# A transformer layer on one core: the order of weighing and turning in attention, the first products, and matmuls ahead of the last scaling

## The chip, the cores and the metric

The kernel runs on one core of one Trainium2 chip. Its five engines each work through their own list of instructions: TensorE (PE; its weight loads are shown as PEld) multiplies matrices into the accumulator memory PSUM, VectorE (DVE), ScalarE (ACT) and GpSimd (POOL) do the elementwise work, and SyncE (SP) issues the DMA transfers between the chip's main memory and the on-chip memory. Semaphores order them against one another. The metric is the device time of one execution in microseconds (us).

## The reference

One layer of an encoder over two request groups that share the weights (512 and 1024 tokens, width 1024), all in float32:

```python
a = _rmsnorm(h, norm_mix_g)
z = a @ w_in                                  # q, k, v and u, 1280 columns
o_attn = _attention(q, k, v, q_norm_g, k_norm_g)   # 8 heads, 2 for k and v, axial rotary, softmax
o_pool = _pool_mixer(u, w_pool, pool_scale)
h = h + jnp.concatenate([o_attn, o_pool], axis=-1) @ w_out
m = _rmsnorm(h, norm_mlp_g)
h = h + jnp.square(jax.nn.relu(m @ w_up)) @ w_down
gate = jax.nn.sigmoid((_rmsnorm(h, norm_ple_g) @ w_ple_gate).astype(jnp.float32)).astype(h.dtype)
h = h + gate * (p_i @ w_ple_proj)
return _rmsnorm(h, final_norm_g)
```

## The kernel before

Every operand of a product is split into a high part (rounded to the type fp32r) and a low part (the rest), and a product of two operands is three products on PE: high by high, high by low, low by high. The splitting (a copy or cast on ACT, a subtraction on DVE or POOL) is most of the elementwise work. The order of PE, ACT, DVE and POOL is written out by hand; SP's follows the order in which loads and stores are written and the semaphores that they wait for. Data tiles lie in 49 equal slots that are handed on as they come free.

**Start.** Eight bf16 products of a constant tile (`warm`) run on PE while the first data comes. The tokens lie in 12 tiles of 128. `z` of a tile is a sum over 8 blocks `k` of 128 input features, and a block is nine products: six of 512 columns (weights `W1`, two column ranges) and three of 256 (weights `W2`). `mm_k(t, k)` issues the nine products of tile t and block k. Tiles 0 and 1 run together over k, since the weights only arrive then: `load_w(k)` issues the loads, `split_w(k)` splits the weights (ACT, then DVE), `load_x` and `split_x` do the same for the tokens. Of tiles 0 and 1 the features of blocks 0 and 1 (`head`) come first, the rest (`tail`) later.

**Attention.** A unit is one tile of 128 queries with the 4 query heads of one k/v head. The loop over `at` works in rounds, four to a unit. A round issues the score `S` of one head (`score`; DVE takes its maximum), the exponential of the round before (`soften`, ACT), its division by the sum (`norm`, POOL), the turn of finished probabilities `pr` (`turn`: four PE transposes into a PSUM buffer `tp` for each 128 keys; there are two such buffers), the split of the turned ones into `pt` (`split`: high part on ACT, rest on DVE, which frees the buffer), and the weighing of the values with the `pt` of the round before (`weigh`: PE adds into the accumulator `o`). A unit of the first request group has 4 key tiles, one turned in each round; a unit of the second has 8, two in each round. A round can end with a piece of other work from the queue `fill`: of `pool_out` (products `pp`, first 48 pieces of six products) or of `heads_out` (products `po`, 12 of 256 columns, for a pair of tiles whose heads are done). In the rounds with `at` from 62 to 95 a piece is taken only in some even ones. Where the variable `filled` is true, a round weighs first and then turns; otherwise it turns first. It is true from round 3 on as long as `fill` holds anything, whether or not the round takes a piece.

**End.** After the MLP and the gate, the last group of tokens (256) is normalised in `finish`. `rsqrt_rows` sums the squares `sq` over the features on PE (`ss`), in two parts since the last one comes late, raises the mean to the power -1/2 (DVE, POOL), puts it on a diagonal (`dg`, DVE) and spreads it to all partitions with one product (`bc`). DVE then multiplies five parts of the result by `bc`, which lies in PSUM, and SP stores each.

Of the kernel before, what the change touches and what calls it, by code (L numbers as in the profile page):

```python
# [9 lines left out]
F32 = mybir.dt.float32  # L10
F32R = mybir.dt.float32r
AF = mybir.ActivationFunctionType
ALU = mybir.AluOpType
# [22 lines left out]
def encoder_layer(ctx, tc, xT, xn, xr, pT, w1, w2, w_pool, w_out, w_up, w_down, w_gate, w_proj,  # L36
# [18 lines left out]
    def load(dst, src):  # L55
        ins = sy.dma_start(dst, src).ins
        if last_pe[0] is not None:
            tc.add_manual_dep(ins, last_pe[0].name, NOSYNC, reason="not before its turn")
# [79 lines left out]
    w2raw = {}  # L138
    gmix_sb = const.tile([P, KD], F32, name="gmix_sb")

    def load_w(k):
        raw = slot([P, D], F32, f"w1r{k}")
        for part in ([slice(0, CH), slice(CH, D)] if k == 0 else [slice(0, D)]):
            load(raw[:, part], w1[k][:, part])
        if k % 2 == 0:
            w2raw[k // 2] = slot([P, 2, 256], F32, f"w2r{k}")
            load(w2raw[k // 2], w2[k // 2])
            w2t = slot([P, 2, 2, 256], F32R, f"w2_{k}")
            W2[k], W2[k + 1] = [[w2t[:, b, i] for i in range(2)] for b in range(2)]
        W1[k] = [slot([P, D], F32R, f"w1_{k}_{i}") for i in range(2)]  # L150
        return raw, w2raw[k // 2][:, k % 2]

    def split_w(k, raws):
        g = gmix_sb[:, k:k + 1]
        parts = [(raws[0], W1[k]), (raws[1], W2[k])]
        if k == 0:
            parts[:1] = [(raws[0][:, h], [w[:, h] for w in W1[k]]) for h in (slice(0, CH), slice(CH, D))]
        for r, W in parts:
            sc.activation(W[0], r, AF.Copy, scale=g)  # L159
            ve.scalar_tensor_tensor(W[1], r, g, as32(W[0]), op0=ALU.mult, op1=ALU.subtract)  # L160

# [1 line left out]
    wz = slot([P, CH], mybir.dt.bfloat16, "warm")  # L163
    gp.memset(wz, 1.0)
    wps = tp_ps("warm")
    for i in range(8):
        pe.matmul(wps, wz[:, 0:P], wz, start=True, stop=True)
    ones_sb = const.tile([P, P], F32R, name="ones_sb")
    gp.memset(as32(ones_sb), 1.0)
# [1 line left out]
    load(gmix_sb, g_mix)  # L171
    head, tail = slice(0, 2), slice(2, KD)
    x0 = load_x(0, (head,))
    raws = [load_w(0)]
    x1 = load_x(1, (head,))
    raws += [load_w(1)]
    for t, x in ((0, x0), (1, x1)):
        load(x[:, tail], xT[t][:, tail])
        raws.append(load_w(2 + t))
    split_x(0, x0, head)  # L180
    split_w(0, raws[0])
    split_x(1, x1, head)
    split_w(1, raws[1])
    split_x(0, x0, tail)
    split_w(2, raws[2])
# [42 lines left out]

    zs = {}

    def mm_k(t, k):
        if k == 0:
            zs[t] = ps("z", f"z{t}")
        z = zs[t]
        hi = [(i, j, 0) for j in range(3) for i in range(2)] if k == 0 and t < 2 else [(i, j, 0) for i in range(2) for j in range(3)]
        lo = [(0, j, 1) for j in range(3)]
        for i, j, w_ in (hi[:3] + lo + hi[3:] if k else hi + lo):
            w = W2[k][w_] if j == 2 else W1[k][w_][:, j * CH:(j + 1) * CH]
            pe.matmul(z[:, j * CH:min((j + 1) * CH, 1280)], xt[t][i][:, k, :], w,
                      start=k == 0 and i + w_ == 0, stop=k == KD - 1 and i == 1)  # L240
# [331 lines left out]
    def step(n=1):  # L572
# [5 lines left out]
        while n and chores:  # L578
            try:
# [2 lines left out]
            except StopIteration:  # L582
                chores.popleft()

    def rsqrt_rows(parts, w, name):

        n = w // P
        ss = tp_ps(f"ss{name}")
        for i, part in enumerate(parts):
            for b in range(n):  # L590
                pe.matmul(ss[:, b:b + 1], part[:, b * P:(b + 1) * P], as32(ones_sb[:, 0:1]),
                          start=i + b == 0, stop=i == len(parts) - 1, skip_group_check=True)
        r = small.tile([P, 4], F32, tag="rs", name=f"rs{name}", bufs=2)
        ve.tensor_scalar(r[:, :n], ss[:, :n], 1.0 / D, EPS, op0=ALU.mult, op1=ALU.add)
        if name in ("g0", "g1"):
            yield
        gp.tensor_tensor(r[:, :n], r[:, :n], mhalf[:, :n], op=ALU.pow)
        spread = [P, n, P]
        if len(parts) > 1:
            dg = slot([P, w], F32, f"dg{name}")  # L600
            ve.tensor_tensor(dg.rearrange("p (a b) -> p a b", a=n), id_sb.unsqueeze(1).to_broadcast(spread),
                             r[:, :n].unsqueeze(2).to_broadcast(spread), op=ALU.mult)
            bc = tp_ps(f"bc{name}")
            pe.matmul(bc[:, :w], as32(ones_sb), dg, start=True, stop=True)
            return bc[:, :w]
        rh = small.tile([P, 2, 4], F32R, tag="rh", name=f"rh{name}", bufs=2)
        gp.tensor_scalar(rh[:, 0, :n], r[:, :n], 1.0, 1.0, op0=ALU.mult, op1=ALU.mult)
        gp.tensor_tensor(rh[:, 1, :n], r[:, :n], as32(rh[:, 0, :n]), op=ALU.subtract)
        dg = slot([P, 2, w], F32R, f"dg{name}")
        if name in ("g0", "g1"):  # L610
            yield from wait(2)
        for i in range(2):
            ve.tensor_tensor(dg[:, i].rearrange("p (a b) -> p a b", a=n), id_sb.unsqueeze(1).to_broadcast(spread),
                             as32(rh[:, i, :n]).unsqueeze(2).to_broadcast(spread), op=ALU.mult)
        yield from wait({"f20": 4, "g2": 8, "f00": 7, "f10": 4}.get(name, 3))
        bc = tp_ps(f"bc{name}")
        for i in range(2):
            pe.matmul(bc[:, :w], ones_sb, dg[:, i], start=i == 0, stop=i == 1)
        return bc[:, :w]
# [594 lines left out]
            at_join(n, join_product, g, h)  # L1214
            at_join(n + 3, join_store, g, h)
    start_chunk(0)
    for k in range(KD - 2):
        mm_k(0, k)
        mm_k(1, k)
    mm_k(0, KD - 2)  # L1220
# [75 lines left out]
    for at in range(2, 4 * len(units) + 6):  # L1296
# [26 lines left out]
        if last:  # L1323
            last[0].norm(last[1])
            if last[1] == 3:
                n = last[0].n
                turning += [[(last[0], kt) for kt in range(i * n // 4, (i + 1) * n // 4)] for i in range(4)]
        filled = bool(fill) and at >= 3
        if filled:
            done = [un_ for un_, kt in lag if un_.weigh(kt)]  # L1330
        for un_, kt in fresh:
# [5 lines left out]
        if not filled:  # L1337
            done = [un_ for un_, kt in lag if un_.weigh(kt)]

        n = 0 if at < 3 else 2 - at % 2 if at < first_sample else 1  # L1340
        took = n and bool(fill)
        for i in range(max(n, 1)):
            if i == n - 1 or not n:
# [347 lines left out]
    def finish(c, o, w, sq):  # L1691
        tok = slice(o, o + w)
        if not o:
            yield from wait((2, 4, 3)[c])
        bc = yield from rsqrt_rows(sq, w, f"f{c}{o}")
        if o:
            for a, part in ((0, slice(0, 1)), (0, slice(1, 2)), (1, slice(0, 2)), (2, slice(0, 2)), (3, slice(0, 2))):
                h = res(c, 2 * a + part.start, tok, 2)[:, 0:part.stop - part.start]
                ve.tensor_tensor(h, h, bc.unsqueeze(1).to_broadcast([P, part.stop - part.start, w]), op=ALU.mult)
                sy.dma_start(y_out[c, a][:, part, tok], h)  # L1700
            return
        r = slot([P, w], F32, f"fr{c}{o}")
        sc.copy(r, bc)
        yield from wait(2)
        for a in range(4):
            for e in range(2):
                h = res(c, 2 * a + e, tok)
                ve.scalar_tensor_tensor(h, h, gfin_sb[:, 2 * a + e:2 * a + e + 1], r, op0=ALU.mult, op1=ALU.mult)  # L1708
                if not e:
                    yield  # L1710
            sy.dma_start(y_out[c, a][:, :, tok], hT[c][a][:, :, tok] if c < 2 else res(c, 2 * a, tok, 2))
            yield
# [127 lines left out]
```

## Time and profile before

| | |
|---|---|
| median of 3 runs | 1744.55 us (1744.01 to 1744.94) |
| the profiled execution | 1746.53 us |
| its span, first to last instruction | 1744.8 us |
| mean granted TensorE clock | 0.997 |
| first products of z | from 5.48 us |
| rounds of attention | 186 to 536 us |
| MLP | 561 to 1592 us, overlapping the gate |
| gate and last norm | 1543 to 1745 us |

All times in the profile count from the start of the span. A row of the timeline gives start, duration, engine, line, operation, out<-in, shape and count, and in brackets the idle time before it with what ended it. Rows of the same operation are drawn together while the engine does not stand still. A row of the list of waits gives who waited for whom, the total, how often, and the longest. A row of the windows gives the stretch and its length, then busy time and (count) of each engine, the granted clock, the DMA engines' share and GB/s. A row of the groups gives the count, the busy time in total, the mean duration in ns, and the idle time before them. The ends of matmuls are modelled: of a stream of matmuls the starts tell more than the durations.

### The profile page before, as it was taken

What the parts mean: (1) busy time and instruction counts of PE and PEld (TensorE: products, weight loads), DVE (VectorE), ACT (ScalarE), POOL (GpSimd) and SP (SyncE); (2) the same over time, 40 slices, a digit from 0 to 9 for tenths busy, and PEclk for the clock granted to TensorE, in tenths of its full rate; (3) what the DMA queues carried; (4) which work ended last, traced back from release to release, by engine and by line L of the source; (5) the groups of instructions that cost most, each with busy time, mean ns of one, the idle gap of its engine ahead of it and who ended that gap; (6) DMA issues with size and microseconds to landing.
All of it is one profiled execution on the core that took longest, in us unless ns stands there. A gap on an engine that the chain in (4) does not pass through costs nothing. (4 is left out here: it accounts for less than half of the span.)

```text
span 1744.8 us, 31256 instructions
## 1 busy us (share of the span) xinstructions
PE 1716.8 (98%) x11684; PEld 1568.6 (90%) x11684; DVE 1262.5 (72%) x1724; ACT 886.9 (51%) x1605; POOL 1072.9 (61%) x870
## 2 busy tenths in 40 slices
PE   9999999999999999999999999999999999999997
PEld 7888878888878998888989999999999999998897
DVE  5777765777886668677757777777778788675666
ACT  5454354667885545554445455544454445533233
POOL 1585984434665766868546677866588577653422
PEclk9999999999999999999999999999999999999998
DMA  7354745120428887979797978779776888853012
GB/s 257 133 203 161 264 159 190 63 97 13 145 79 334 305 298 266 364 287 349 295 377 286 351 240 328 270 279 368 253 262 244 298 284 315 295 188 115 13 49 97
DMA packets 137063, 400.16 MB, mean 229 GB/s; under 512 B 14544, under 2 KB 27216, under 8 KB 136912
## 3 DMA queue, kind: packets, MB, share of 16 engines
q1 hardware_dynamic: 136912, 398.17, 62.6%
q8 instruction: 92, 1.51, 0.3%
q14 instruction: 59, 0.48, 0.1%
HBM read 280.15 MB, written 117.96 MB: 228 GB/s over the span
## 5 line engine op out<-in xcount | busy, mean ns | idle before, releaser
L49 PE MATMUL pd<-ta,v 128*128 128x256 f32 x2688 | 338.4, 282 | 0.1
L49 PEld LDWEIGHTS pd<-ta,v 128*128 128x128 f32 x2688 | 328.3, 190 | 0.7 <-POOL v L1098 0.3
L1098 POOL TENSOR_TENSOR v<-we,v 128x512 fp32r<-128x512 f32 x128 | 184.8, 1465 | 102.0 <-DVE ta L1118 37.8
L49 PE MATMUL pd<-r,wd 128*128 128x512 f32 x768 | 189.7, 395 | 1.6 <-DVE r L1015 1.3
L1098 POOL TENSOR_TENSOR v<-vs,v 128x512 fp32r<-128x512 f32 x96 | 127.5, 1350 | 96.9 <-DVE c L1121 32.5
L49 PE MATMUL z<-w,x 128*128 128x512 f32 (+1 forms) x864 | 176.8, 362 | 1.7 <-ACT w L159 1.7
L505 POOL TENSOR_SCALAR pr<-pr,rr 128x1024 f32<-128x1024 f32 (+1 forms) x96 | 94.7, 987 | 134.7 <-DVE rr L503 72.2
L1118 DVE TENSOR_TENSOR ta<-c,ta 128x512 fp32r<-128x512 f32 x112 | 116.9, 1044 | 78.0 <-ACT ta L1116 73.8
L49 PEld LDWEIGHTS z<-w,x 128*128 128x128 f32 x864 | 145.0, 191 | 28.6 <-ACT w L159 3.6
L49 PEld LDWEIGHTS pd<-r,wd 128*128 128x128 f32 x768 | 139.7, 188 | 31.4 <-DVE r L1015 3.1
L909 POOL TENSOR_TENSOR w<-ws,w 128x512 fp32r<-128x512 f32 x72 | 107.8, 1498 | 93.5 <-ACT w L908 87.3
L49 PE MATMUL pq<-mo,w 128*128 128x256 f32 x1152 | 152.3, 281 | 5.1 <-DVE c L1050 2.9
L49 PE MATMUL pz<-mo,w 128*128 128x256 f32 x1152 | 152.6, 282 | 0.8 <-DVE u L1045 0.8
L49 PE MATMUL px<-mo,w 128*128 128x256 f32 x1152 | 152.5, 282 | 0.0
L49 PEld LDWEIGHTS pz<-mo,w 128*128 128x128 f32 x1152 | 145.7, 189 | 4.1 <-DVE u L1045 1.2
L49 PEld LDWEIGHTS pq<-mo,w 128*128 128x128 f32 x1152 | 143.1, 189 | 6.1 <-DVE c L1050 3.3
L49 PEld LDWEIGHTS px<-mo,w 128*128 128x128 f32 x1152 | 144.4, 189 | 1.4
L515 ACT CAST pt<-tp 128x512 fp32r<-128x512 f32 x160 | 87.8, 590 | 111.4 <-PE tp L53 109.7
L49 PE MATMUL pg<-hg,wg 128*128 128x512 f32 (+1 forms) x768 | 141.2, 338 | 0.2 <-DVE hg L1438 0.2
L516 DVE TENSOR_TENSOR pt<-tp,pt 128x512 fp32r<-128x512 f32 x160 | 104.2, 685 | 48.1 <-ACT pt L515 48.1
L49 PEld LDWEIGHTS pg<-hg,wg 128*128 128x128 f32 x768 | 119.2, 188 | 17.0 <-DVE hg L1438 0.4
L489 DVE TENSOR_REDUCE nm<-S 128x1 f32<-128x1024 f32 (+1 forms) x96 | 100.1, 1043 | 22.4 <-PE S L49 21.9
(257 smaller groups left out, 3506.7 us busy)
## 6 DMA issues: line engine op xcount, KB each, us to landing
w<-kept_d SPq DMA_DIRECT2D x210, 512.0 KB, 6.0
kept_d<-w SPq DMA_DIRECT2D x105, 512.0 KB, 4.4
we<-in_w_down_dram SPq DMA_DIRECT2D x64, 512.0 KB, 6.8
mo_d<-mm SPq DMA_DIRECT2D x84, 256.0 KB, 5.8
mo<-mo_d SPq DMA_DIRECT2D x42, 512.0 KB, 10.0
wur<-in_w_up_dram SPq DMA_DIRECT2D x36, 512.0 KB, 8.2
wdr<-in_w_down_dram SPq DMA_DIRECT2D x32, 512.0 KB, 6.4
h_d<-h SPq DMA_DIRECT2D x16, 512.0 KB, 2.9
```

The costliest lines, as they stand in the source:

```text
L49: last_pe[0] = nc.tensor.matmul(*a, **k).ins
L489: ve.tensor_reduce(nm, S[:, :nch * CH], axis=AX.X, op=ALU.max, negate=True)
L505: gp.tensor_scalar(p, p, rr, 1.0, op0=ALU.mult, op1=ALU.mult)
L515: sc.copy(self.pt[kt][:, 0], tp)
L516: ve.tensor_tensor(self.pt[kt][:, 1], tp, as32(self.pt[kt][:, 0]), op=ALU.subtract)
L909: gp.tensor_tensor(t[:, 1], x, as32(t[:, 0]), op=ALU.subtract)
L1098: ins = gp.tensor_tensor(lo[:, p], src[:, p], as32(hi[:, p]), op=ALU.subtract).ins
L1118: last_ve[0] = ve.tensor_tensor(t[:, 1], x, as32(t[:, 0]), op=ALU.subtract).ins
```

## The change

Four places change.

- The first products. `mm_first` replaces the first blocks of tiles 0 and 1. It goes by column ranges: all six products on `W1` of tile 0, then of tile 1, then the three on `W2` of each. Tile 1's load is issued ahead of the load of `W2`, and its split ahead of that of `W2`. The number of `warm` products goes from 8 to 10.
- Attention. `filled` is now true only in rounds that will take a piece of `fill`; all other rounds turn first and weigh after. Round 3 takes two pieces in place of one.
- `rsqrt_rows` issues 14 products of `ones_sb` with itself (128 columns) between the two parts of the sum, and 11 ahead of the product that spreads it, in the one call that has two parts.
- `finish`: for the last group ACT copies the spread factors to `r`, and POOL multiplies the last part (two feature tiles of 256 tokens) by `r`, while DVE does the other four. Its store is issued fourth.

```diff
-    def load_w(k):
+    def load_w(k, between=lambda: None):
         raw = slot([P, D], F32, f"w1r{k}")
         for part in ([slice(0, CH), slice(CH, D)] if k == 0 else [slice(0, D)]):
             load(raw[:, part], w1[k][:, part])
+        W1[k] = [slot([P, D], F32R, f"w1_{k}_{i}") for i in range(2)]
+        other = between()
         if k % 2 == 0:
...
-    def split_w(k, raws):
+    def split_w(k, raws, between=lambda: None):
...
         for r, W in parts:
+            if W is W2[k]:
+                between()
             sc.activation(W[0], r, AF.Copy, scale=g)
...
-    for i in range(8):
+    for i in range(10):
         pe.matmul(wps, wz[:, 0:P], wz, start=True, stop=True)
...
-    raws = [load_w(0)]
-    x1 = load_x(1, (head,))
+    raws = [load_w(0, lambda: load_x(1, (head,)))]
+    x1 = raws[0][2]
...
-    split_w(0, raws[0])
-    split_x(1, x1, head)
+    split_w(0, raws[0], lambda: split_x(1, x1, head))
...
+    def mm_first():
+        for js in ((0, 1), (2,)):
+            for t in range(2):
+                if t not in zs:
+                    zs[t] = ps("z", f"z{t}")
+                for i, j, w_ in [(i, j, 0) for j in js for i in range(2)] + [(0, j, 1) for j in js]:
+                    w = W2[0][w_] if j == 2 else W1[0][w_][:, j * CH:(j + 1) * CH]
+                    pe.matmul(zs[t][:, j * CH:min((j + 1) * CH, 1280)], xt[t][i][:, 0, :], w,
+                              start=i + w_ == 0, stop=False)
...
+    def keep_warm(n, name):
+        wp = ps_g("g", name)
+        for _ in range(n):
+            pe.matmul(wp[:, 0:P], ones_sb, ones_sb, start=True, stop=True)
...
         for i, part in enumerate(parts):
+            if i:
+                keep_warm(14, f"wa{name}")
...
+            keep_warm(11, f"wb{name}")
             bc = tp_ps(f"bc{name}")
...
-    for k in range(KD - 2):
+    mm_first()
+    for k in range(1, KD - 2):
         mm_k(0, k)
         mm_k(1, k)
...
-        filled = bool(fill) and at >= 3
+        filled = bool(fill) and at >= 3 and (at < 62 or at % 2 == 0 and (at < 76 or at % 3 or len(fill) > 10) or at >= 96)
...
-        n = 0 if at < 3 else 2 - at % 2 if at < first_sample else 1
+        n = 0 if at < 3 else 2 if at == 3 else 2 - at % 2 if at < first_sample else 1
...
         if o:
-            for a, part in ((0, slice(0, 1)), (0, slice(1, 2)), (1, slice(0, 2)), (2, slice(0, 2)), (3, slice(0, 2))):
+            r = slot([P, w], F32, f"fr{c}{o}")
+            sc.copy(r, bc)
+            for a, part in ((0, slice(0, 1)), (3, slice(0, 2)), (0, slice(1, 2)), (1, slice(0, 2)), (2, slice(0, 2))):
+                e, by = (gp, r) if a == 3 else (ve, bc)
                 h = res(c, 2 * a + part.start, tok, 2)[:, 0:part.stop - part.start]
-                ve.tensor_tensor(h, h, bc.unsqueeze(1).to_broadcast([P, part.stop - part.start, w]), op=ALU.mult)
-                sy.dma_start(y_out[c, a][:, part, tok], h)
+                e.tensor_tensor(h, h, by.unsqueeze(1).to_broadcast([P, part.stop - part.start, w]), op=ALU.mult)
+                if a != 3:
+                    sy.dma_start(y_out[c, a][:, part, tok], h)
+                if a == 1:
+                    sy.dma_start(y_out[c, 3][:, :, tok], res(c, 6, tok, 2))
```

How the order on PE changes at three places. First, PE's first products of z, before. `z_433` is tile 0, `z_443` tile 1; `w_0_0` and `w_0_1` are the high and low parts of `W1`, `w_0_123` is `W2`; `x_0` and `x_1` are the high and low parts of a tile's tokens.

```order
L49 MATMUL z_433<-w_0_0_124,x_1_146 128x512
L49 MATMUL z_433<-w_0_123,x_0_145 128x256
L49 MATMUL z_433<-w_0_123,x_1_146 128x256
L49 MATMUL z_433<-w_0_1_125,x_0_145 128x512 x2
L49 MATMUL z_433<-w_0_123,x_0_145 128x256
L49 MATMUL z_443<-w_0_0_124,x_0_155 128x512
```

The same place after the change, where `z_435` is tile 0 and `z_442` tile 1, from the last high product on `W1` of tile 0:

```order
L49 MATMUL z_435<-w_0_0_123,x_1_148 128x512
L49 MATMUL z_435<-w_0_1_124,x_0_147 128x512 x2
L49 MATMUL z_442<-w_0_0_123,x_0_155 128x512
L49 MATMUL z_442<-w_0_0_123,x_1_156 128x512
L49 MATMUL z_442<-w_0_0_123,x_0_155 128x512
L49 MATMUL z_442<-w_0_0_123,x_1_156 128x512
L49 MATMUL z_442<-w_0_1_124,x_0_155 128x512 x2
L49 MATMUL z_435<-w_0_129,x_0_147 128x256
```

The products on `W2` stood fifth, ahead of eight products on `W1`; now they stand behind all of those.

Second, PE in a round late in attention that takes no piece of `fill` (`at` is 71), from the last product of its score, before:

```order
L49 MATMUL S_13_4994<-ks_1_1611,qb_4353 128x512
L49 MATMUL o_0_4984<-pt_02_4976,vs_941 128x512 x2
L49 MATMUL o_0_4984<-pt_03_4979,vs_941 128x512 x2
L53 MATMUL tp_04_5008<-id_sb,pr_00_4774 128x128
L53 MATMUL tp_04_5008<-id_sb,pr_01_4813 128x128
L53 MATMUL tp_04_5008<-id_sb,pr_02_4849 128x128
L53 MATMUL tp_04_5008<-id_sb,pr_03_4883 128x128
L53 MATMUL tp_05_5013<-id_sb,pr_00_4774 128x128
L53 MATMUL tp_05_5013<-id_sb,pr_01_4813 128x128
L53 MATMUL tp_05_5013<-id_sb,pr_02_4849 128x128
L53 MATMUL tp_05_5013<-id_sb,pr_03_4883 128x128
L49 MATMUL S_00_5032<-ks_0_939,qb_4738 128x512
```

And after:

```order
L49 MATMUL S_13_4996<-ks_1_1613,qb_4355 128x512
L53 MATMUL tp_04_5006<-id_sb,pr_00_4776 128x128
L53 MATMUL tp_04_5006<-id_sb,pr_01_4815 128x128
L53 MATMUL tp_04_5006<-id_sb,pr_02_4851 128x128
L53 MATMUL tp_04_5006<-id_sb,pr_03_4885 128x128
L53 MATMUL tp_05_5011<-id_sb,pr_00_4776 128x128
L53 MATMUL tp_05_5011<-id_sb,pr_01_4815 128x128
L53 MATMUL tp_05_5011<-id_sb,pr_02_4851 128x128
L53 MATMUL tp_05_5011<-id_sb,pr_03_4885 128x128
L49 MATMUL o_0_4986<-pt_02_4978,vs_943 128x512 x2
L49 MATMUL o_0_4986<-pt_03_4981,vs_943 128x512 x2
L49 MATMUL S_00_5034<-ks_0_941,qb_4740 128x512
```

The weighing of key tiles 2 and 3 moved behind the turn of key tiles 4 and 5. The same holds in all 15 rounds that take no piece between `at` 71 and 93, in round 95, whose weighing then stands directly ahead of round 96's, and in round 52, whose piece was taken a round earlier. From round 3 to round 52 each piece of `fill` after the first stands one place earlier in the queue than before; where two pieces share a round, the rounds' pieces read alike.

Third, PE's end, before (`ssf` is the sum of squares, `bcf` the spread product):

```order
L49 MATMUL pg_19832<-hg_1_19142,wg_0_18585 128x256
L49 MATMUL pg_19832<-hg_0_19141,wg_1_18586 128x256
L49 MATMUL ssf_19870<-ones_sb,s_19546 128x1 x2
L49 MATMUL ssf_19870<-ones_sb,s_19860 128x1 x2
L49 MATMUL bcf_19880<-dgf_19878,ones_sb 128x256
```

And after:

```order
L49 MATMUL pg_19834<-hg_0_19143,wg_1_18588 128x256
L49 MATMUL ssf_19872<-ones_sb,s_19548 128x1 x2
L49 MATMUL waf_19875<-ones_sb 128x128 x14
L49 MATMUL ssf_19872<-ones_sb,s_19862 128x1 x2
L49 MATMUL wbf_19897<-ones_sb 128x128 x11
L49 MATMUL bcf_19909<-dgf_19895,ones_sb 128x256
```

One new group stands ahead of the second ssf, the other ahead of bcf.

More of the change, by code (lines that the diff above doesn't have):

```diff
@@ L149, in load_w @@
             W2[k], W2[k + 1] = [[w2t[:, b, i] for i in range(2)] for b in range(2)]
-        W1[k] = [slot([P, D], F32R, f"w1_{k}_{i}") for i in range(2)]
-        return raw, w2raw[k // 2][:, k % 2]
-    def split_w(k, raws):
+        return raw, w2raw[k // 2][:, k % 2], other
+    def split_w(k, raws, between=lambda: None):
         g = gmix_sb[:, k:k + 1]
@@ L234, in mm_k @@
         z = zs[t]
-        hi = [(i, j, 0) for j in range(3) for i in range(2)] if k == 0 and t < 2 else [(i, j, 0) for i in range(2) for j in range(3)]
+        hi = [(i, j, 0) for i in range(2) for j in range(3)]
         lo = [(0, j, 1) for j in range(3)]
```

## The prediction

> **What bounds the kernel now.** I read the page's busy line first, then the list of waits for TensorE (PE, and its weight loads PEld).
>
> ```profile
> PE 1716.8 (98%) x11684; PEld 1568.6 (90%) x11684; DVE 1262.5 (72%) x1724; ACT 886.9 (51%) x1605; POOL 1072.9 (61%) x870
> ...
> PE z L49 <- ACT w L159: 1.7, 2, 1.2
> ...
> PE S L49 <- ACT pr L499: 0.9, 1, 0.9
> ...
> PEld o L49 <- DVE pt L516: 12.5, 37, 1.3
> ```
>
> TensorE is busy for 98% of the span, so time comes off only where it stands still or runs slowly: at the start (z waits for w), at the start of attention (S waits for pr), in 37 places where the weighing product `o` waits for the split probabilities `pt`, and after the last product. The change touches just these. All else keeps its order, so what is won at the start or in attention moves everything behind it forward.
>
> **Start.** The rows are from the timeline, from windows over it, and from the groups.
>
> ```profile
> 1.34 3.60 PE L49 MATMUL warm<-warm 128*128 128x512 bf16 x8 [1.34 <-POOL warm L164]
> 5.48 2.07 PE L49 MATMUL z<-w,x 128*128 128x512 f32 x4 [0.55 <-ACT w L159]
> 8.17 0.51 ACT L159 ACTIVATE w<-w2r,gmix_sb 128x256 fp32r<-128x256 f32 x1 [1.99 <-DMA w2r<-in_w_dram]
> 12.20 0.48 DVE L160 SCALAR_TENSOR_TENSOR w<-w2r,gmix_sb,w 128x256 fp32r<-128x256 f32 x1
> ...
> 8.73:13.59 4.86, 4.86 (x15) 1.00 1.03 404
> ...
> L49 PE MATMUL z<-w,x 128*128 128x512 f32 (+1 forms) x864 | 176.8, 362 | 1.7 <-ACT w L159 1.7
> ```
>
> Four 512-column products take 2.07 us here, 0.52 each; a block of nine (six of 512 columns, three of 256) takes 176.8 / 96 = 1.84 us over the kernel. The first 18 products run at about half speed: 14 of them fill 8.73 to 13.59. Tile 0 is through its second weight block at 13.59 + 1.84 = 15.4. After the change two more warm products (0.45 each) close the 0.55 us gap, and the 1.17 us wait for w2 is filled with the low parts of tile 0 and the first products of tile 1; tile 1's load goes past one load on SP, and its cast past w2's on ACT, where ACT was idle for 1.99. Next is late the weight data: the second block's last low part is there at 12.20 + 0.48 = 12.68, and 4 of 9 products come behind it (0.8 us), so tile 0 is through at 13.5. That is 1.9 us sooner if the clock has risen by then. With the clock up early, the first 18 products are through about 1 us behind w2's split (8.17 + 0.51), and PE then waits for data for some 2 of the 3 us to 12.68. If the clock falls in that gap, one stretch of 3.4 us at half speed gives 1.7 back. I take 1.4, with ends at 0 and 1.9.
>
> That a partly idle stretch can halve the clock is shown at the other end of the kernel:
>
> ```profile
> 1730.69:1734.10 3.41, 1.94 (x16) 1.65 (x14) 2.89 (x8) 1.35 (x4) 0.79 (x1) 1.00 0.37 128
> 1734.10:1737.50 3.40, 1.44 (x5) 1.35 (x6) 1.33 (x4) 0.92 (x2) 0.71 (x1) 0.50 0.30 103
> ```
>
> (The columns are busy PE, PEld, DVE, ACT, POOL, then the granted clock.) With PE busy for 1.94 of 3.41 us the clock was halved. [...]
>
> **First rounds of attention.** Round 3 now takes two blocks of pool output.
>
> ```profile
> 201.03 1.64 PE L49 MATMUL pp<-yb,wo 128*128 128x512 f32 x6
> 203.57 0.73 PE L49 MATMUL S<-ks,qb 128*128 128x512 f32 x2 [0.90 <-ACT pr L499]
> ...
> 320.27 0.77 PE L53 MATMUL tp<-id_sb,pr 128*128 128x128 f32 x5 [0.50 <-POOL pr L505]
> ```
>
> A further block of six products (1.64 us by its row) covers the 0.90 us wait: the work is only moved. All later blocks come one round earlier, the splits of wo on DVE and POOL with them, so wo's POOL split is no longer right ahead of the pr that tp waits for at 320.27. The round that loses its block may wait for the DVE instead. I take 1.0, ends 0.2 and 1.4.
>
> **The late rounds.** A round is S (score), o (weigh), tp (turn) and sometimes po (a fill block of 12). The windows count S and po.
>
> ```profile
> 322.29:384.61 62.32, 16.34 (x60) 1.00 0.10 35
> 384.61:390.06 5.45, 2.18 (x9) 1.00 0.72 248
> 423.19:446.33 23.14, 8.80 (x32) 1.00 0.03 12
> 446.33:530.26 83.93, 27.34 (x97) 1.00 0.37 132
> ...
> 446.33:530.26 83.93, 14.79 (x108) 1.00 0.37 132
> ```
>
> Four S make a round. The first window is 15 rounds with a fill block, 4.15 us each. The next two are rounds without one, which already turn before they weigh: two of 2.72 and eight of 2.89 us. The last has 24 rounds, 9 with fill (108 / 12) and 15 without, which weigh first. Priced like the others, it would take 9 x 4.15 + 15 x 2.72 = 78.2 or, with 2.89, 80.7 us in place of 83.93. Why it costs more:
>
> ```profile
> 473.64 1.17 PE L49 MATMUL S<-ks,qb 128*128 128x512 f32 x4
> 474.65 1.62 PE L49 MATMUL o<-pt,vs 128*128 128x512 f32 x4
> 476.11 1.04 PE L53 MATMUL tp<-id_sb,pr 128*128 128x128 f32 x8
> ...
> PEld o L49 <- DVE pt L516: 9.7, 32, 0.6
> ...
> PEld tp L53 <- DVE pt L516: 1.4, 4, 0.6
> ```
>
> Here o stretches over 1.46 us, where S takes 1.01: between a turn and the weighing of it stand only the 0.9 us of S, less than ACT's copy and two DVE splits need. This window has 32 waits of o for DVE, the eight turn-first rounds only 4 of tp. After the change o stands in between too (S, tp, o, S, then the next use): the splits have 1.8 us. The turn's own buffers come free with the same splits, so it gains as much in a row of such rounds; behind a fill block they have long been free. A round with fill that follows a turn-first round finds its pt ready also. What can stop this are the engines that split:
>
> ```profile
> 423.19:446.33 23.14, 22.98 (x130) 18.31 (x129) 20.54 (x35) 21.48 (x41) 16.69 (x15) 1.00 0.03 12
> 446.33:530.26 83.93, 83.06 (x494) 66.67 (x492) 68.74 (x119) 67.98 (x129) 52.68 (x48) 1.00 0.37 132
> ```
>
> In the eight turn-first rounds ACT is busy for 93%, which makes them 2.89. Over the late window DVE and ACT have 68 to 69 us of work, so 79.7 us holds it at 86%, and runs of three rounds without fill will be near 2.89, single ones at 2.72. I take 4.2; ends 0 and 5.7.
>
> At the end of the rounds two weighings follow one turn directly:
>
> ```profile
> 533.37 0.49 PE L49 MATMUL o<-pt,vs 128*128 128x512 f32 x1 [0.24 <-ACT pt L515]
> 534.09 1.10 PE L49 MATMUL o<-pt,vs 128*128 128x512 f32 x3 [0.23 <-DVE pt L516]
> ```
>
> Four products from 533.37 to 535.04 are 1.67 us for 0.92 of work. Now four other products stand between. I take 0.7, ends 0 and 0.8.
>
> **End.**
>
> ```profile
> 1732.13 0.61 PE L49 MATMUL ssf<-ones_sb,s 128*128 128x1 f32 x4
> 1734.56 1.01 PE L49 MATMUL ssf<-ones_sb,s 128*128 128x1 f32 x4 [1.82 <-ACT s L1683]
> 1737.07 1.22 PE L49 MATMUL bcf<-dgf,ones_sb 128*128 128x256 f32 x2 [1.50 <-DVE dgf L601]
> 1738.33 2.54 DVE L1699 TENSOR_TENSOR H<-H,bcf 128x256 f32<-128x256 f32 x5 [1.31 <-PE bcf L49]
> 1738.82 2.81 SPq L1700 DMA_DIRECT2D out_dram<-H  x5
> ...
> L1689 POOL TENSOR_TENSOR s<-s,s 128x512 f32<-128x512 f32 x14 | 19.2, 1369 | 59.7 <-ACT s L1683 59.6
> ...
> L53 PE MATMUL tp<-id_sb,pr 128*128 128x128 f32 x640 | 86.3, 273 | 0.7 <-POOL pr L505 0.5
> ```
>
> The second ssf takes 1.01 us with the halved clock, the first 0.61; bcf takes 1.22 and should halve. Kept at full clock they save 0.4 + 0.6. The price is 14 and 11 products of 128 columns, of a type that the trace does not show at this width. By the turns they take 86.3 / 640 = 0.135 each: 14 are 1.9 us in a gap of 1.82, 11 are 1.5 in a gap of 1.50, so both just fit. At 0.25 each (the four 512-column S from 473.64 to 474.65) they would be 1.7 and 1.3 too late. [...] For the last scaling, ACT copies bcf (0.4) and POOL scales one part of 512 columns (1.37), done 1.8 after bcf; DVE does 1.9 us in place of 2.54, but SP issues five outputs in 2.81, one after the other, and waits for POOL ahead of the last: 0.2 of this arrives. Sum 0.9, ends -1.7 and 1.3.
>
> **Sum.** 1.4 + 1.0 + 4.2 + 0.7 + 0.9 = 8.2 us off the profiled execution's 1746.53 (span 1744.8 and 1.7 around it), which makes 1738.3. The median of the runs is 1744.55, 2.0 lower, so I forecast 1736.4.
>
> **Rivals.**
> - *Small gain.* The clock falls again (0.3), every round costs 2.89 (3.2), the end gives nothing, the rest 1.0: 4.5 us, 1740.0. For it: ACT's 93%. Against: single rounds stand alone.
> - *Splits become the bound.* The turn takes over o's waits, and the late rounds give nothing: 8.2 - 4.9 = 3.3 at best, with no gain at the end 2.4: 1742.2. This also covers a change that doesn't do what it says, and a gain that the first MLP loads take back.
> - *Slower.* If what releases the turn (POOL's pr or DVE's split) comes at the time at which it turns now, each of the 15 rounds waits for the 0.92 us of S or o that stood ahead of it: 15 x 3.64 + 37.4 = 92 us, 8.1 more. Less 3.3 from elsewhere that is 4.8 slower, 1749.4. It decides from releases that come over 0.4 us after S ends. Against it: 1.4 us of such waits in eight rounds.
> [...]
>
> **How the numbers follow.** Forecast 0.50, clock staying up 0.10, small gain 0.18, splits the bound 0.15, slower 0.07. A measurement tells about 0.2%, 3.5 us: the first three are faster (0.78), the fourth is the same (0.15), the last slower (0.07). The range goes from 1732.0 (all upper ends, 1.9 + 1.4 + 5.7 + 0.8 + 1.3 = 11.1, and 1.4 more for runs that differ) to 1742.5, which takes in the fourth case's best and leaves out the last and the rest of the fourth.
>
> **What would show it.** Right: the second block's z products start before 13 us; no wait of S for pr in the first rounds; late rounds near 2.72 and 4.15, with few waits of o for DVE pt; bcf at 0.6 us and a clock of 1.00 to the end. Wrong: tp waiting for DVE pt or POOL pr in each late round, a second slow stretch after 12 us, or ssf starting late behind the 14 products.

## The result and the profile after

| | before | after |
|---|---|---|
| median | 1744.54 us of 8 runs (1743.47 to 1746.31) | 1739.79 us of 8 runs (1737.84 to 1741.32) |
| ratio of the two | | 0.9972, 95% interval 0.9961 to 0.9982 |
| profiled execution | 1746.53 us, span 1744.8 | 1738.3 us, span 1736.4 |

The change saves 4.75 us (3.1 to 6.8 by the interval), where the forecast had 8.2. The two profiled executions differ by just those 8.2 us, but the one of before was slower than each of the eight timed runs, and the one of after is the second fastest of its own. Most of what follows is about this difference.

The busy line of the page of after, and its list of waits for PE and PEld (what waits, for what, us in all, times, the longest):

```profile
PE 1715.4 (99%) x11711; PEld 1572.3 (91%) x11711; DVE 1257.7 (72%) x1723; ACT 887.5 (51%) x1606; POOL 1074.4 (62%) x871
```

```profile
PE pq L49 <- DVE c L1070: 2.8, 1, 2.8
...
PE z L49 <- ACT w L162: 0.9, 2, 0.7
...
PE z L49 <- DVE w L163: 0.5, 1, 0.5
...
PEld o L49 <- DVE pt L528: 3.1, 7, 0.7
PEld tp L53 <- DVE pt L528: 3.0, 10, 0.6
```

The waits of `o` for `pt` are down from 12.5 us in 37 places to 3.1 in 7, `tp` waits 3.0 instead of 1.4, and the wait of `S` for `pr` is gone. In the 24 late rounds, where before had 9.7 us of waits of `o` for `pt`, only the turn still waits for `pt`, 1.6 us in 6 places:

```profile
PEld tp L53 <- DVE pt L528: 1.6, 6, 0.5
```

The late rounds, by windows from the first S of the round `at` = 71 to that of 95, as before, and the fill blocks `po` among them (the second row, a view of `po` alone):

```profile
442.37:521.74 79.37, 79.26 (x493) 68.43 (x492) 69.07 (x120) 68.20 (x129) 53.27 (x48) 1.00 0.38 140
```

```profile
442.37:521.74 79.37, 14.83 (x108) 13.35 (x108) 3.35 (x8) 1.00 0.38 140
```

The same 24 rounds, with the same 108 products of fill, take 79.37 us in place of 83.93. This is 4.56 us less, where the prediction had 4.2. DVE and ACT have as much work as before, 69 and 68 us.

The start, by the timeline of PE:

```profile
5.41 0.74 PE L49 MATMUL z<-w,x 128*128 128x512 f32 x2
6.33 3.85 PE L49 MATMUL z<-w,x 128*128 128x512 f32 x16 [0.19 <-ACT w L162]
10.85 0.85 PE L49 MATMUL z<-w,x 128*128 128x512 f32 x3 [0.68 <-ACT w L162]
12.17 4.00 PE L49 MATMUL z<-w,x 128*128 128x512 f32 x19 [0.47 <-DVE w L163]
```

The first 18 products are through at 10.18, and then PE waits for the split of the second block. The clock rose at 4.97 us in this execution and did not fall in these gaps.

The end, by windows (the last columns are granted clock, DMA share and GB/s) and by the timeline:

```profile
1725.29:1728.70 3.41, 2.99 (x25) 2.71 (x24) 1.95 (x6) 0.93 (x2) 0.71 (x1) 1.00 0.45 152
1728.70:1732.11 3.41, 0.87 (x2) 0.15 (x1) 1.95 (x4) 0.37 (x1) 1.27 (x1) 0.50 0.21 71
```

```profile
1724.44 1.76 PE L49 MATMUL waf<-ones_sb 128*128 128x128 f32 x14
...
1726.40 0.61 PE L49 MATMUL ssf<-ones_sb,s 128*128 128x1 f32 x4 [0.21 <-ACT s L1704]
...
1726.87 1.42 PE L49 MATMUL wbf<-ones_sb 128*128 128x128 f32 x11
...
1728.50 1.06 PE L49 MATMUL bcf<-dgf,ones_sb 128*128 128x256 f32 x2 [0.21 <-DVE dgf L620]
1729.60 0.37 ACT L1719 COPY fr<-bcf 128x256 f32<-128x256 f32 x1 [2.71 <-PE bcf L49]
1730.01 1.95 DVE L1723 TENSOR_TENSOR H<-H,bcf 128x256 f32<-128x256 f32 x4 [1.56 <-ACT fr L1719]
```

The 14 and 11 products fit into their gaps, but PE was busy for 2.99 of 3.41 us and the clock was halved all the same, in the middle of `bcf`. And DVE now waits for ACT's copy of `bcf` ahead of its first multiply, which it did not before: 0.45 us from the end of `bcf` (1728.50 + 1.06) to 1730.01, against 0.04 before (1737.07 + 1.22 to 1738.33).

Where the profiled pair gains, from the PE times of each tile in the two traces (`px` and `pq` are products of the MLP, `pg` those of the gate, `qp` turns queries ahead of a unit):

| stretch | before | after | gain |
|---|---|---|---|
| to the first S of attention | 186.34 | 184.38 | 1.96 |
| from there to the first S of round `at` = 71 | 259.99 | 257.99 | 2.00 |
| the 24 late rounds | 83.93 | 79.37 | 4.56 |
| from there to the first `px` of the MLP | 30.41 | 29.68 | 0.73 |
| `px` to the start of the last `pg` | 1171.08 | 1172.17 | -1.09 |
| from there to the end of the span | 13.01 | 12.78 | 0.23 |

### The profile page after: what moved, and what is told of

Its sections match the earlier page's. It is cut to its first block, busy times and chain, and to the rows that moved or that the text cites. A ratio compares the mean times of both kernels' runs of the same rounds, so it can differ in the third digit from the quotient of the medians.

```text
span 1736.4 us, 31309 instructions
## 1 busy us (share of the span) xinstructions
PE 1715.4 (99%) x11711; PEld 1572.3 (91%) x11711; DVE 1257.7 (72%) x1723; ACT 887.5 (51%) x1606; POOL 1074.4 (62%) x871
```

## The experiments

Four kernels with one part of the change each, then four and four more; those of one set were timed on the same chip, beside runs of before. Medians are given as the difference from the median of before in the same set, with the 95% interval of the ratio in us.

**Only the rule for rounds without a fill block** (before, with one line):

```diff
-        filled = bool(fill) and at >= 3
+        filled = bool(fill) and at >= 3 and (at < 62 or at % 2 == 0 and (at < 76 or at % 3 or len(fill) > 10) or at >= 96)
```

> Only the rule for weighing ahead of a turn is changed. My theory: this rule carries over half of the gain, 4.6 us in the late rounds and 0.7 in the two weighings behind the last round, so the median is 5.3 below the kernel before, 1739.2 (1738.5 to 1740.0), the rounds without a fill block take 2.71 to 2.75 us, and the start and the first rounds are those of before. Rival, that the gain is given back later: the score products of the MLP start 5.3 sooner, but the median is only 2 to 3 below, since the MLP takes as much longer as it starts sooner.

Measured: 1741.60 against 1745.39, 3.8 less (1.9 to 5.1), between the two expectations. The late rounds of this kernel, by windows:

```profile
444.39:523.74 79.35, 79.23 (x493) 68.48 (x492) 69.04 (x120) 68.22 (x129) 53.34 (x48) 1.00 0.38 140
```

They take 79.35 us, to 0.02 what the whole change has, so the rule alone makes the 4.56. From the first S to the first `px` are 368.96 us in place of 374.33, 5.4 less. The median gains 1.6 less than that, and 5.4 lies just above its interval. In this profile the first `px` to the start of the last `pg` take 1173.29 us against 1171.08 in that of before, with one stretch at half clock that the latter does not have. Whether a part of the gain is given back there in most runs, as the rival has it, is not shown.

**Only the start**: the order of loads and splits, ten warm products, `mm_first`.

> Only the start is changed (the order of loads and splits, ten warm products, first products of two tiles by columns). My theory: the start saves 1.96 us where the clock rises near 5 us and stays up, as in the one profile of the changed kernel, but in most runs it falls once more in the gap near 10 us or rises one stretch of 3.4 us later, which costs 1.7; so the median is 0.3 to 1.2 below the kernel before, about 1743.7, and the five runs spread over 2 us. Rival, that the clock does the same in each run: median 1742.6, spread under 1 us.

Measured: 1745.33 against 1745.39, 0.06 less (from 1.4 faster to 1.7 slower). The rival falls, and so do the number of my theory (0.3 to 1.2 below) and its reason: the clock of this execution rose at 4.66 and did not fall at the start, and the first S still came only at 184.57. The table below shows that the old start is as early.

**Only the second block in round 3:**

```diff
-        n = 0 if at < 3 else 2 - at % 2 if at < first_sample else 1
+        n = 0 if at < 3 else 2 if at == 3 else 2 - at % 2 if at < first_sample else 1
```

> Only the second block of pool output in round 3 is changed. My theory: 2.2 us come from here, as the two profiles show between round 3 and round 53, so the median is 1742.3 (1741.9 to 1742.8). Rival: most of that came from the profiled execution of before being a late one, and only the wait of 0.9 us that the block covers is won: 1743.6.

Measured: 1743.19 against 1745.39, 2.2 less (0.9 to 3.8), as the theory had it. PE's waits from 184 to 390 us, of before and then of this kernel:

```profile
PE S L49 <- ACT pr L499: 0.9, 1, 0.9
PE o L49 <- DVE pt L516: 0.9, 1, 0.9
PE qp L53 <- DVE pt L516: 0.8, 1, 0.8
PE tp L53 <- POOL pr L505: 0.5, 1, 0.5
PE S L49 <- DVE vs L275: 0.3, 1, 0.3
```

```profile
PE o L49 <- DVE pt L516: 0.7, 3, 0.3
PE S L49 <- DVE vs L275: 0.3, 1, 0.3
PE pp L49 <- DMA yb<-yT_d: 0.3, 1, 0.3
PE qp L53 <- DVE pt L516: 0.3, 1, 0.3
```

Not only the 0.9 of `S` is gone, but also the 0.5 of `tp` for POOL, and 0.5 of `qp`.

**Only the end**: the products to keep the clock up, and the shared scaling.

> Only the end is changed (products that should keep the clock up, and the last scaling shared by DVE and POOL). My theory: the products of 128 columns do not keep the clock up, which falls at the end of a stretch of 3.4 us as before, and the rest saves 0.3 us: median 1744.2 (1743.9 to 1744.6). Rival, that the clock stays up except where the phase of the stretches is unlucky: 0.9 to 1.3 saved, 1743.4.

Measured: 1746.71 against 1745.39, 1.3 more (from 0.5 faster to 2.8 slower). No gain is shown; neither expectation had a loss. Of its profile's length 1.0 us lies where this kernel changes nothing: from the first S to the first `px` are 375.33 us against 374.33, as the one wait of `tp` for POOL's `pr` there takes 1.6 us in place of 0.5.

**The whole change again, and two versions of it.** The second has products in two idle places of the MLP (in `run7`, which works on a pair of feature blocks; pairs 6 and 12 of the third token chunk), into an accumulator that is free there:

```diff
+            if self.id in {'2_6': 3, '2_12': 10}:
+                wm = ps("u", f"wm{self.id}")
+                for _ in range({'2_6': 3, '2_12': 10}[self.id]):
+                    pe.matmul(wm, ones_sb, ones_sb.unsqueeze(1).to_broadcast([P, 4, P]), start=True, stop=True)
             self.product(4, q, False)
```

The third has wide products at the end:

```diff
-        wp = ps_g("g", name)
+        wp = ps_g("g", name)[:, 0:CH]
+        wide = ones_sb.unsqueeze(1).to_broadcast([P, 4, P])
...
-            pe.matmul(wp[:, 0:P], ones_sb, ones_sb, start=True, stop=True)
+            pe.matmul(wp, ones_sb, wide, start=True, stop=True)
...
-                keep_warm(14, f"wa{name}")
+                keep_warm(6, f"wa{name}")
...
-            keep_warm(11, f"wb{name}")
+            keep_warm(5, f"wb{name}")
```

> The changed kernel once more, as the base for the next two and a second look at its clock. My theory: the runs of this kernel differ by the clock, which is halved for one or two stretches of 3.41 us where such a stretch lies over the idle 2.9 us of TensorE near 1461 to 1464 us (pq waits for DVE c) or over the start; median 4 to 5 below the kernel before, spread 2 to 4 us. Rival: the spread comes from transfers in the MLP, and the clock is the same in all runs.

> The changed kernel with 10 products of 512 columns in the idle 2.9 us before pq in pair 12 of the third token chunk (near 1461 us), and 3 in that of pair 6 (near 1338 us). My theory: the clock never falls there, so the median is 1.0 to 1.5 below the changed kernel of the same call, no run has a mean clock under 0.997, and the spread gets smaller. Rival: the clock falls for other reasons or in few runs; median within 0.5 of the changed kernel.

> The changed kernel with 6 and 5 products of 512 columns in place of 14 and 11 of 128 at the end. [...] Rival: the clock falls whatever is in there, and the end stays 12.8 or becomes longer, as the last of six wide products may still run when the second ssf could start.

And the two changes in attention without those at the start and the end:

> The two changes in attention alone (the rule for weighing ahead of a turn, and the second block in round 3); start and end as before. My theory: start and end gave nothing in the median (0.0 and -1.3 in their own runs), so this is as fast as the whole change or up to 1 us faster: 5 to 6 below the kernel before. Rival: the start is worth 1.9, as the two first profiles seem to show, so this is 1.5 to 2 slower than the whole change of the same call.

Measured, against 1745.61 in this set: the whole change 1740.40, 5.2 less (2.4 to 6.5); with the products in the MLP 1738.56; with wide products at the end 1739.29; attention alone 1737.98, 7.6 less (5.1 to 9.4). The spread of the whole change is 4.7 us (1737.97 to 1742.68), over the 2 to 4 of the theory, and its profile has the clock halved for one stretch at 1464.30, as the theory had it. With the products in the MLP it is 1.8 lower, a little more than expected; no run has a mean clock under 0.997, but the spread is still 3.7. With the wide products the clock was at 1.00 up to 1733.39, behind `bcf`, but from the last `pg` to the end are 12.45 us, as in the whole change of this set (12.50), so no gain at the end is shown. Attention alone gained more than was expected of it: the change without its start and end is 2.4 faster than with them. The intervals overlap, but the next set gave 7.3 (4.4 to 8.7) for attention alone.

**Attention alone, with the products in the MLP, and two ends:**

> The two changes in attention alone once more, as the base for the next three. My theory: start and end of the change give nothing, so this is again 5.5 to 7.5 below the kernel before; its clock still falls near 1461 us in most runs. Rival: its first result was a lucky set of five runs, and it is no faster than the whole change (4.7 to 5.2 below).

> The two changes in attention, and the 13 products of 512 columns in the two idle places of the third token chunk. My theory: the fall of the clock near 1461 us costs 1.7 us in three runs of four, and it is gone, so the median is 1.0 to 1.7 below the kernel without them, and the profile shows a clock of 1.00 from the start to the last products. Rival: the products only take the place of idle time, and the median is the same within 0.5.

> As the one before, with the last scaling shared by DVE and POOL, and nothing else of the change at the end. My theory: five outputs are still issued by SP one after the other, so this saves 0 to 0.4 from the last scaling on, and the median does not differ by more than 0.5. Rival: the shared scaling is what gains at the end, 0.6 to 1.0, and was hidden by the products that keep the clock up.

> As the one before, with 6 and 5 products of 512 columns ahead of the second ssf and of bcf. My theory: the clock stays at 1.00 until bcf in most runs, and from the last pg to the end are 12.4 us or less, against 12.3 to 13.1 with the end of before; median 0.3 to 0.6 below the kernel without them. Rival: they delay ssf or bcf when the clock falls inside them, and the median is the same or up to 1 us later.

Measured, against 1744.55 in this set: attention alone 1737.25 (1736.58 to 1737.53); with the products in the MLP **1735.67** (1734.05 to 1736.68), the lowest median of all, ratio to before 0.9952 (0.9939 to 0.9966); with the shared scaling too 1736.69; with wide products at the end as well 1735.91. The medians that the theories gave for the first two hold; the clock of the second was at 1.00 from 10.40 us on and fell at 1727.31. For the third neither expectation came true, since its median is 1.0 higher, not equal and not lower, though the runs overlap. The fourth gains 0.8 on the third and is 0.2 above the second, and its end of 12.61 us misses the 12.4 of its theory: by these medians, the wide products pay for what the shared scaling costs, and no more.

**The first S, in all 14 traces.** The second column is the time from which the record of the granted clock has 1.00. Ahead of it products run at about half the pace: in before one of 512 columns starts every 0.43 us up to 13.59 and every 0.23 from 13.92. Where a stretch is named, the clock is at 0.50 in it. The fourth column runs from the first S to the first `px`, the last from the start of the last `pg` to the end of the span:

| kernel | full clock from | first S | to first `px` | last `pg` to end |
|---|---|---|---|---|
| before | 13.78 | 186.34 | 374.33 | 13.01 |
| rule only | 9.26 | 184.39 | 368.96 | 13.11 |
| block only | 5.26 | 183.71 | 372.56 | 12.29 |
| end only | 4.06, halved 7.47 to 10.88 | 184.72 | 375.33 | 12.54 (new end) |
| attention alone | 4.31 | 184.84 | 366.41 | 12.59 |
| attention alone, again | 5.35 | 183.49 | 366.53 | 12.59 |
| and products in the MLP | 10.40 | 184.11 | 366.63 | 12.28 |
| and shared scaling | 4.44, halved 7.85 to 11.27 | 184.37 | 366.71 | 13.46 (scaling new) |
| and wide products at the end | 10.25 | 183.89 | 366.47 | 12.61 (wide) |
| **new start:** whole change | 4.97 | 184.38 | 367.04 | 12.78 (new end) |
| whole change, again | 6.80 | 184.54 | 367.22 | 12.50 (new end) |
| with products in the MLP | 5.38 | 185.06 | 367.48 | 13.68 (new end) |
| with wide products at the end | 6.25 | 184.12 | 367.49 | 12.45 (wide) |
| start only | 4.66 | 184.57 | 374.52 | 12.58 |

The upper nine kernels have the start of before. Only the first of them, the profile on which the prediction was made, has a late first S. The other eight reach it at 183.49 to 184.84 (mean 184.19), as the five with the new start do (184.12 to 185.06, mean 184.53). How the old start runs when the clock rises early, by the timeline of PE of the kernel with the second block only:

```profile
5.45 4.29 PE L49 MATMUL z<-w,x 128*128 128x512 f32 x18 [0.52 <-ACT w L159]
10.24 0.85 PE L49 MATMUL z<-w,x 128*128 128x512 f32 x3 [0.50 <-ACT w L159]
11.57 4.78 PE L49 MATMUL z<-w,x 128*128 128x512 f32 x23 [0.47 <-DVE w L160]
```

Here too PE ends by waiting for the split of the second weight block, and goes on at 11.57, sooner than the new start (12.17). In the nine traces in which the clock was up by 9.3 us and stayed up, the 22nd product starts within 0.07 us of the end of that split (in the other five 0.12 to 1.98 us behind it). The split ends at 11.29 to 12.65 with the old order (mean 11.87 of nine) and at 11.90 to 12.76 with the new one (mean 12.27 of five). The split of the second block bounds the start, and ACT stands idle for its weights ahead of it (0.78 us in the whole change, 1.59 in the kernel with the block only); two warm products and an order by columns did not bring it sooner.

**The clock in the MLP.** In 8 of the 10 traces without products there, the clock is halved for one stretch of 3.41 us or two, behind the one wait of 2.8 to 2.9 us in which `pq` waits for DVE's `c`. Windows of 3.41 us over this wait, first of before (whose clock stayed at 1.00 up to 1734.10; the window ends 77 such lengths ahead of that), then of the rule only, then of attention alone in its second run, where the second window begins at the fall:

```profile
1467.86:1471.27 3.41, 1.77 (x15) 1.57 (x14) 3.41 (x4) 0.00 (x0) 2.69 (x3) 1.00 0.26 108
```

```profile
1463.34:1466.75 3.41, 0.86 (x7) 0.86 (x8) 2.82 (x5) 0.52 (x2) 2.88 (x3) 1.00 0.46 154
1466.75:1470.16 3.41, 3.41 (x18) 3.41 (x18) 2.56 (x3) 1.77 (x3) 2.13 (x2) 0.50 0.94 325
1470.16:1473.57 3.41, 3.41 (x31) 3.41 (x31) 1.21 (x4) 2.85 (x5) 1.63 (x2) 1.00 1.04 404
```

```profile
1459.43:1462.84 3.41, 1.48 (x12) 1.48 (x13) 2.21 (x4) 1.13 (x3) 3.41 (x3) 1.00 0.62 189
1462.84:1466.25 3.41, 3.41 (x18) 3.41 (x18) 2.99 (x4) 1.24 (x3) 2.13 (x3) 0.50 0.98 368
```

A stretch at half clock holds 18 products in place of 31. (The kernel with the block only has one more, at 0.50 from 1343.28 to 1346.70, behind a wait for weights kept in memory.) The windows lie over the wait in another way in each execution: PE was busy for 1.77 us in the one behind which the clock stayed, and for 0.86 and 1.48 in those behind which it was halved. That this decides whether it comes is an estimate from these windows. The same kernel, attention alone, without and with the ten wide products in that wait, by the timeline:

```profile
1461.36 1.77 PE L49 MATMUL pq<-mo,w 128*128 128x256 f32 x12 [2.84 <-DVE c L1050]
1462.93 2.77 PE L49 MATMUL px<-mo,w 128*128 128x256 f32 x12
```

```profile
1459.62 2.44 PE L49 MATMUL wm<-ones_sb 128*128 128x512 f32 x10
1462.62 1.69 PE L49 MATMUL pq<-mo,w 128*128 128x256 f32 x12 [0.57 <-DVE c L1050]
1464.15 1.59 PE L49 MATMUL px<-mo,w 128*128 128x256 f32 x12
```

The first is halved 1.5 us after the wait and `px` takes 2.77; in the second `px` takes 1.59. None of the four kernels with these products has the fall. Two of them have the same kernel without beside them, and their medians are 1.8 and 1.6 us lower (1738.56 against 1740.40, 1735.67 against 1737.25); in both pairs the runs overlap, in the second in one run only.

**The clock at the end.** Windows over the last products: the change with products in the MLP, whose end has the 128-column products, and then the kernel with 512-column products:

```profile
1725.70:1729.11 3.41, 3.09 (x26) 2.75 (x25) 2.53 (x7) 1.34 (x3) 0.27 (x1) 1.00 0.47 156
1729.11:1732.53 3.42, 3.22 (x13) 2.49 (x12) 0.58 (x2) 0.17 (x1) 0.71 (x1) 0.50 0.24 80
```

```profile
1723.74:1727.15 3.41, 3.02 (x15) 1.92 (x13) 2.08 (x6) 1.01 (x3) 0.71 (x1) 1.00 0.38 125
1727.15:1730.56 3.41, 0.70 (x2) 0.30 (x2) 2.10 (x5) 0.37 (x1) 1.27 (x1) 1.00 0.31 105
```

With about the same busy time in the first window (3.09 and 3.02 us) the clock was at 0.50 behind the narrow products and at 1.00 behind the wide ones, which made `bcf` 0.70 in place of 1.06 (after) or 1.22 (before). What the narrow ones cost when the clock falls in them, by the timeline of the first of these two kernels:

```profile
1728.93 2.44 PE L49 MATMUL wbf<-ones_sb 128*128 128x128 f32 x11
1731.16 1.16 PE L49 MATMUL bcf<-dgf,ones_sb 128*128 128x256 f32 x2
```

The eleven take 2.44 us, where the whole change has 1.42, `bcf` stands behind them though `dgf` was there at 1730.51, and its end is 13.68 us long, the longest of all.

The ends differ also by where in them the clock falls, so they are compared here where that is the same. It falls 5.3 us after the start of the last `pg` in two traces with the end of before, which take 12.28 and 12.29 us, and 5.4 us after it in two with the new end, which take 12.54 and 12.50. It falls at 3.5 to 3.6 us in three with the end of before (12.58 to 12.59) and in the one of 13.68 with the new end. It falls at 2.9 and 3.0 us in the kernel with the rule only (13.11) and in the one with the shared scaling alone (13.46). Each time the end with a new part is the longer one, by 0.2 to 1.1 us.

## Why the prediction was right or wrong

The range, the sign and the mechanism in attention were right; the forecast of the time was 3.4 us too low. Start and end, 2.3 of the 8.2 us, gave nothing or a loss, and the three terms of attention, 7.3 us in the traces where 5.9 were forecast, made up for a part of it.

| term | predicted | shown |
|---|---|---|
| start | 1.4 (0 to 1.9) | 0.06 by its own kernel; the first S 0.3 later by the means of eight and five traces |
| first rounds | 1.0 (0.2 to 1.4) | 2.2 by its own kernel, 2.00 in the traces, above the upper end |
| late rounds | 4.2 (0 to 5.7) | 4.56 in the traces |
| two weighings behind the rounds | 0.7 (0 to 0.8) | 0.73 in the traces, 0.80 with the rule only (30.41 - 29.61) |
| end | 0.9 (-1.7 to 1.3) | 0.23 in the profiled pair; -1.3 (-2.8 to 0.5) by its own kernel; -0.2 to -1.1 where the clock falls at the same point |

- **Start.** The step that failed is "That is 1.9 us sooner if the clock has risen by then": it set a new start with an early clock against an old one with a late clock, and took the second as a property of the kernel. It was that execution's. With an early clock the old start waits for the same split of the second block, which the prediction had named as "next late". The case of a clock that stays up there, to which the prediction gave 0.10, was that of this execution (1.00 from 4.97 on), and its gain, the upper end of 1.9, did not come for the same reason; with the start of before the clock fell again at the start in two of nine traces (at 7.47 and 7.85 us), with the new one in none of five. In the nine kernels with the start of before the full clock began anywhere from 4.06 to 13.78 us, so one execution says little of a term that rests on it.
- **First rounds.** Right in kind, under-sized. The prediction saw that the 0.90 of `S` and the 0.50 of `tp` could go, and held some back as the round that loses its block might wait for DVE instead; the list shows waits of at most 0.3 for it, and 0.5 of the wait of `qp` for DVE went as well, which the sum does not have.
- **Late rounds.** Right in mechanism and size. In the profile of after the rounds without fill are at 2.71 to 2.76 us, three of them at 2.92 to 3.23, those with fill at 4.13 to 4.16, one at 4.31, from the times of S; the rival that the turn takes over all the waits of `o` falls (`tp` waits for `pt` in 6 places there, 1.6 us in all).
- **End.** Two steps failed. "Kept at full clock they save 0.4 + 0.6": the second `ssf` took 0.61 as said, but the clock still fell, and `bcf` saved 0.16; of the prediction's own signs, "bcf at 0.6 us and a clock of 1.00 to the end" did not come. The 1.01 and 1.22 us to be saved were also those of one execution, whose clock fell 2.4 us after the start of the last `pg`; where it falls at 5.3, the same end takes 12.28 us in place of 13.01 without any change. And of the shared scaling "0.2 of this arrives": DVE's first multiply waits for ACT's copy, and from the end of `bcf` to its start are 0.4 us more. From that multiply to the end of the span it saved only 0.06 (6.42 before, 6.36 after). The sum, 0.40 + 0.16 - 0.40 + 0.06 = 0.22, is the 0.23 of the table but for 0.01. The trace shows the wait (1.56 us idle, ended by ACT `fr`); why DVE waits there, though it reads `bcf` and not `fr`, is not shown.
- **The sum.** The forecast's 8.2 is also the difference of the two profiled executions, by luck: that pair had 1.96 for the start, which only the late clock of the one gave, and lost 1.09 from the first `px` to the last `pg`, for which the prediction ("All else keeps its order") had no term. The rival *Small gain* (4.5 us, 1740.0) is within 0.3 us of what was measured, also by luck: it was right that the end gives nothing, but it had every round without fill at 2.89 us, and most of them are at 2.71 to 2.76. With the late rounds 4.56 us shorter, the rivals *Splits become the bound* and *Slower* fall.

What stays open: by the medians of one set, attention alone was 2.4 us faster than the whole change, and no single stage shows all of it. The first S comes 0.3 later with the new start, by the means above. Between the first S and the first `px` the five kernels with the old start and both attention changes take 366.41 to 366.71, the four with the new start 367.04 to 367.49, 0.8 more by the means; but the kernel with the end only is 1.0 above before in this stretch, with the same start. From the first `px` to the last `pg`, six traces have no stretch at half clock: four with the old start take 1170.71 to 1172.06, two with the new one 1172.17 and 1173.10. The ends in the profiles of that set, 12.50 us for the whole change and 12.59 for attention alone, do not explain it. That the start is the cause in any of these stretches is not shown.

## What to carry to other kernels

A gain that rests on the clock or on where it changes has to be read from several executions: the same start had its full clock anywhere from 4 to 14 us, and one profile, here of an execution slower than all timed runs, made a term out of that. Before a start or an end is rearranged, ask what it waits for once the clock is up; here it was the second weight block. Wide products in the one long wait of the MLP gave 1.6 to 1.8 us by medians of five and six runs, more than start and end together, and the parts in attention with these products have the lowest median of all versions here.

## What the hardware showed that was not expected

- Where the clock of PE was halved and came back, it was so for 3.41 us (1466.75 to 1470.16 in the kernel with the rule only) or for two such lengths (1468.98 to 1475.81 in the one with the start only). The first rise came at another time in each execution, from 4.06 to 13.78 us. And the clock fell without PE being idle for all of the 3.41 us before: it was halved behind 0.86 us (the rule only) and 1.48 us (attention alone) of 256-column products in them, and not behind 1.77 (before).
- The busy time in the profile doesn't tell these cases apart: 3.09 us of 3.41 with mostly narrow products was followed by half clock, 3.02 with wide ones was not. At the start, 1.93 us mostly of 512-column products (4.44 to 7.85 in the kernel with the shared scaling) were followed by half clock, though 1.77 us of 256-column ones in the MLP were not. A product of 128 columns starts every 0.111 us (`waf` and `wbf` in the profile of after), one of 512 every 0.231 (`S` in its late rounds), so a column costs the narrow one almost twice the time. What it is in these windows that the clock goes by is not shown.
